# The mixer of a hybrid decoder step: column-tiled products merged into longer runs, convolution work in pairs, and the state-space decays loaded ahead

## The chip, the cores and the metric

The kernel runs on one core of a Trainium2 chip. The metric is the device time of one execution in microseconds (us). The kernel before takes 1382.97 us (median of three runs, 1382.23 to 1383.33). One of its executions was profiled; all durations below come from that execution.

## What is computed

The reference is one layer of a decoder, applied to 256 prompt tokens and to 8 sample tokens that continue cached sequences (T = 264 columns in all, D = 2048). Only the first part, the mixer, is touched. It projects the normalised input once, and the columns of the product feed two branches:

```python
proj = rms_norm(x, g_mix) @ w_in                 # [q | k | v | z | x,B,C | dt]
# sliding-window attention, 16 heads of 64, 4 key heads, chunks of 128
p = sink_softmax(logits, mask, sinks);  o = p @ v
# state-space branch (SSD), 32 heads of 64 in 4 groups, chunks of 128
xbc = silu(causal_dwconv(xbc, conv_w, conv_b))   # 24 blocks of 128 channels
la = cumsum(dt * a)
decay = exp(la[l] - la[s])                       # l >= s, else 0
y = ((cm @ bm) * decay) @ (xs * dt)              # within a chunk
y += (cm @ h_prev) * exp(la) + xs * d_skip       # from the chunk before
h = h * exp(la_end) + bm @ (xs * dt * decay_end)
y = rms_norm(y * silu(z), norm_g)
```

The concatenated branches go through an output projection. A cross-attention and a gated feed-forward network follow; they are untouched. Beside the result, the new key, value, convolution and state arrays are outputs. For the 8 sample tokens the state update is one step per token from a given state `h0`.

## The kernel before, in words

**The weight stream.** Nearly all of the time is one long stream of matrix products on TensorE (PE). Weights arrive in fp32 in parts of 1024 columns (512 KB) on the DMA queue of SyncE (SP). ScalarE (ACT) casts each part to a high half `whi` (L89), VectorE (DVE) subtracts to get the low half `wlo` (L90), and `mm3` takes three products per 128x128 block: L104 (high by high), L105 (high weights by low activations) and L106 (low weights by high activations). One part feeds 24 products of 264 columns, eight of each line. There are four buffers each for the raw part, `whi` and `wlo`, so the halves can be made at most about four parts ahead of PE, and the load of a part waits until DVE has made the `wlo` four parts earlier. `proj` (L108) walks over the parts; its results are evicted from a PSUM bank by DVE.

**Order.** Each engine executes its own instructions in one fixed order. That order is made at build time by a scheduler; weight work carries high priority, and `tc.issue_after` pins some instructions behind others. Products of the mixer's small work (attention scores, transpositions, values, SSD) stand between the products of the weight stream. PSUM has eight banks: three `mm` and two `t` for projections and small work, and one each of `s`, `x` and `y`.

**Column-tiled products.** Some small products fill only part of PE's columns (64 or 32 of 128): the values of attention (L564, L602), the sums of squares of q (L620), the transposed cumulative sums (L482) and the products of SSD within a chunk (L830). They stand in the order as uninterrupted runs of 2 to 16 instructions; an fp32 product is two instructions.

**The pieces the change touches.** `attn_first` (L568) does the first chunk of two head pairs, with a value run of 8 instructions each, called four times. `attn_prompt` (L525) does the second chunk of one head pair, called eight times, with its own value run. `attn_sample` (L671) does the sample tokens: a root (L287 on ACT, L288 on DVE), copies (L685), scores on PE (L691), maxima (L695), an exponential on ACT (L700), then values. `conv_pair` (L765) evicts two projected blocks into two of four buffers `u` (L739), copies their ends to `cnew` (L746) and convolves them (L748 on ACT, three L750 each on DVE). `ssd_prompt(g)` (L797) handles one group, chunk by chunk: it loads logs of decays by broadcast from DRAM into tiles `e` of 256 KB (L810), makes the decays on ACT (L814 for each head, L815 the exponential), multiplies by the masked product of B and C on DVE (L816), transposes `xs` on PE, runs eight products (16 instructions, L830) into bank `y`, and adds the skip term on DVE (L833, four per chunk). `ssd_sample(g)` (L866) loads states `h` and does a product and a sum for each on DVE (L874, L875). `z_pair` (L890) gates two blocks. The calls stand at L935 to L956:

```python
conv_group(0)
conv_group(1)
ssd_prompt(0)
conv_group(2)
ssd_sample(0)
ssd_prompt(1)
conv_group(3)
```

Of the kernel before, what the change touches and what calls it, by code (L numbers as in the profile page):

```python
# [48 lines left out]
def hybrid_decoder_step_kernel(ctx: ExitStack, tc: tile.TileContext, I, O):  # L49
# [26 lines left out]
    def weights(src, n=2048, into=None):  # L76

        out = []
        with tc.high_priority():
            for o in range(0, n, NPART):  # L80
                w = min(NPART, n - o)
                x = raw_part(w)
                nc.sync.dma_start(out=x, in_=src[:, o:o + w])
# [6 lines left out]
                V.tensor_tensor(out=lo, in0=x, in1=hi.bitcast(F32), op=ALU.subtract)  # L90
                out.append((hi, lo))
# [389 lines left out]
    for c in range(2):  # L481
        PE.matmul(p[0:32, 128 + c * 128:256 + c * 128], dtan[:, c, :], tri, start=True, stop=True)  # L482
# [11 lines left out]
    for i in range(4):  # L494
        u = mp.tile([128, 3 + T], F32, name=f"u{i}")
        P.memset(u[:, 0:3], 0.0)
# [3 lines left out]
    def next_u():  # L500
        ringn[0] += 1
        return ring[ringn[0] % 4]

    laT = next_u()[0:32, 3:259]
    V.tensor_copy(out=laT, in_=p[0:32, 128:384])
    nc.sync.dma_start(out=dram_la.rearrange("c h l -> h c l"), in_=laT.rearrange("p (c l) -> p c l", c=2))
# [18 lines left out]
    def attn_prompt(j, rq, nrq, c):  # L525
# [33 lines left out]
        pt = mp.tile([128, 4, 128], F32, tag="bc", name="pt", bufs=2)  # L559
        S.copy(out=pt[:, 0:2 * nb, :], in_=p[:, 0:2 * nk].rearrange("p (a q) -> p a q", q=128))  # L560
        o = psum("t")
        for h in range(2):
            for kb in range(nb):
                PE.matmul(o[64 * h:64 * h + 64, 0:128], vn[:, kb, pp, 64 * h:64 * h + 64], pt[:, h * nb + kb, :],  # L564
                          start=kb == 0, stop=kb == nb - 1)
        marks["attn"] = S.copy(out=attn[:, j, c * 128:c * 128 + 128], in_=o[:, 0:128])

    def attn_first(j):  # L568
# [29 lines left out]
        S.copy(out=pt, in_=p.rearrange("p (a q) -> p a q", q=128))  # L598
        o = psum("t")
        for i in range(4):  # L600
            h = i % 2
            PE.matmul(o[64 * h:64 * h + 64, 128 * (i // 2):128 * (i // 2) + 128], vn[:, 0, pp, 64 * h:64 * h + 64], pt[:, i, :], start=True, stop=True)  # L602
        S.copy(out=attn[:, j:j + 2, 0:128], in_=o[:, 0:256].rearrange("p (i q) -> p i q", i=2))
# [14 lines left out]
    for d in range(2):  # L618
        for j in range(4):
            PE.matmul(pq[32 * j:32 * j + 32, 0:TP], nw[:, d, :], qsq[d][:, j, :TP], start=d == 0, stop=d == 1)  # L620
# [25 lines left out]
    kl = [mp.tile([128, 2, TP], F32R, tag="e", name="kl", bufs=3) for _ in range(2)]  # L646
# [15 lines left out]

    for j in range(0, 8, 2):
        attn_first(j)
    for j in range(8):
# [3 lines left out]
        attn_prompt(j, rqs[:, :, j % 4, d:d + 2], nrqs[:, :, j % 4, d:d + 2], 1)  # L669

    def attn_sample():  # L671
# [27 lines left out]
        e = mp.tile([128, 129], F32, tag="h0", name="es_e", bufs=3)  # L699
# [7 lines left out]
        dg = mp.tile([128, 128], F32, tag="h0", name="dgs", bufs=3)  # L707
# [29 lines left out]
    def conv_blk(bi, pm):  # L737
        u = next_u()
        V.tensor_tensor(out=u[:, 3:], in0=pm, in1=r0, op=ALU.mult)  # L739
        return u  # L740

    def conv_side(b0, us, dst):
        c = mp.tile([128, 2, TP], F32, tag="c", name="c", bufs=2)
        for m, u in enumerate(us):
            bi = b0 + m
            V.tensor_copy(out=cnew[:, bi, :], in_=u[:, TP:])  # L746
# [18 lines left out]
    def conv_pair(b0, dst):  # L765
        us = []
        in_pair(lambda m, pm: us.append(conv_blk(b0 + m, pm)))
# [27 lines left out]
    xs = quarters("xs")  # L795

    def ssd_prompt(g):  # L797
        hs = slice(8 * g, 8 * g + 8)
        hp = mp.tile([128, 512], F32, tag="hp", name="hp", bufs=1)
        for c in range(2):  # L800
            cs = slice(c * 128, c * 128 + 128)
            p = psum("s")
            PE.matmul(p[:, 0:128], BT[:, g, cs], CT[:, g, cs], start=True, stop=True)
            cbm = p[:, 128:256]
            V.tensor_tensor(out=cbm, in0=p[:, 0:128], in1=tri, op=ALU.mult)
            es = []
            for hh in range(2):
                e = mp.tile([128, 4, 128], F32, tag="e", name="e", bufs=3)
                h0 = 8 * g + 4 * hh
                nc.sync.dma_start(out=e, in_=dram_la[c, h0:h0 + 4, :].partition_broadcast(128))  # L810

                with tc.issue_after(marks["attn"].ins):
                    for j in range(4):
                        S.activation(out=e[:, j, :], in_=e[:, j, :], func=AF.Relu, scale=-1.0, bias=la[:, c * 32 + h0 + j:c * 32 + h0 + j + 1])  # L814
                    S.activation(out=e, in_=e, func=AF.Exp, scale=-1.0)  # L815
                V.tensor_tensor(out=e, in0=e, in1=cbm.unsqueeze(1).broadcast_to([128, 4, 128]), op=ALU.mult)  # L816
                es.append(e)
            p = psum("x")
            for i in range(4):
                tr(p[:, i * 128:i * 128 + 128], xs[g][:, i, cs])  # L820
            xdt = mp.tile([128, 8, 64], F32, tag="xdt", name="xdt", bufs=2)
            V.tensor_tensor(out=xdt, in0=p.rearrange("p (h q) -> p h q", h=8),
                            in1=dtn[:, c, hs].unsqueeze(2).broadcast_to([128, 8, 64]), op=ALU.mult)
            xw = mp.tile([128, 8, 64], F32, tag="bc", name="xw", bufs=2)
            V.tensor_tensor(out=xw, in0=p.rearrange("p (h q) -> p h q", h=8),
                            in1=de[:, c, hs].unsqueeze(2).broadcast_to([128, 8, 64]), op=ALU.mult)
            y = psum("y")
            for h in range(8):
                o = (h % 2) * 64
                PE.matmul(y[o:o + 64, (h // 2) * 128:(h // 2) * 128 + 128], xdt[:, h, :], es[h // 4][:, h % 4, :], start=True, stop=True)  # L830
            x = xs[g][:, :, cs]
            for i in range(4):
                V.scalar_tensor_tensor(out=x[:, i, :], in0=x[:, i, :], scalar=pc("d_skip", 4 * g + i), in1=y[:, i * 128:i * 128 + 128],  # L833
                                       op0=ALU.mult, op1=ALU.add)
            if c == 1:
                yi = psum("y")
                for i in range(4):
                    PE.matmul(yi[:, i * 128:i * 128 + 128], hp[:, i * 128:i * 128 + 128], CT[:, g, cs], start=True, stop=True)
                ti = mp.tile([128, 4, 128], F32, tag="bc", name="ti", bufs=2)
                for h in range(2):  # L840
                    nc.sync.dma_start(out=ti[h * 64:h * 64 + 64], in_=lav[h][4 * g:4 * g + 4, :].partition_broadcast(64))
                S.activation(out=ti, in_=ti, func=AF.Exp)
                V.tensor_tensor(out=ti, in0=yi.rearrange("p (i l) -> p i l", i=4), in1=ti, op=ALU.mult)
                P.tensor_tensor(out=x, in0=x, in1=ti, op=ALU.add)
            st = psum("y")
            PE.matmul(st, Bn[:, c, g, :], xw.rearrange("p h q -> p (h q)"), start=True, stop=True)  # L846
            if c == 0:
                S.copy(out=hp, in_=st)
            else:
# [749 lines left out]
```

## Time and profile before

| what | value |
| --- | --- |
| median of three runs | 1382.97 us (1382.23 to 1383.33) |
| the profiled execution's own time | 1382.65 us |
| its span in the profile | 1380.6 us |
| time outside the span | 2.05 us |
| PE busy | 1375.4 us, 11415 instructions |
| DVE busy | 1050.0 us, 1865 instructions |
| ACT busy | 765.8 us, 1261 instructions |
| DMA moved | 298.32 MB, mean 216 GB/s |

A matrix product is pipelined: the profile gives each a length of about 0.28 us, but the next one starts about 0.12 us after it. What a product costs PE is therefore read from the distance between starts, not from the length in a row. In a row of the timeline stand the start, the length, the engine, the line, the operation, the tile written and the tiles read, the shape and the number of instructions; in brackets the idle time before it and what ended that. The mixer's work on which the change bears lies between about 60 and 420 us of the span.

### The profile page before, as it was taken

How to read it: one execution, taken by the hardware profiler on the slowest of the kernel's cores; microseconds unless marked ns; L12 is line 12 of the kernel's file. 1: busy time of each engine (PE TensorE's matmuls, PEld its weight loads, DVE VectorE, ACT ScalarE, POOL GpSimd, SP SyncE). 2: the span in 40 equal slices, each digit the busy share in tenths (PEclk: the TensorE clock that was granted, in tenths of full speed). 3: DMA queues.
4: the chain of work that ended last, by engine and by line, in shares of the span. 5: the costliest groups of instructions: out<-in, count | busy, mean ns of one | idle time of the engine just before them, and what ended most of it. 6: DMA issues, size and time to landing. Idle time of an engine off the chain costs nothing.

```text
span 1380.6 us, 28767 instructions
## 1 busy us (share of the span) xinstructions
PE 1375.4 (100%) x11415; PEld 1348.0 (98%) x11415; DVE 1050.0 (76%) x1865; ACT 765.8 (55%) x1261; POOL 96.1 (7%) x286
## 2 busy tenths in 40 slices
PE   9999999999999999999999999999999999999999
PEld 8999999999999999899999999999999999999998
DVE  7979799999987784579777765776577657765655
ACT  7667756556545555566565544554455445543532
POOL 0000011111000000002010000000000000000000
PEclk9999999999999999999999999999999999999999
DMA  7954468777677576865676766676567656656554
GB/s 297 333 161 134 147 209 254 228 247 256 227 230 240 185 232 213 303 235 198 190 260 214 257 215 186 212 260 213 185 214 244 198 183 198 198 183 185 193 186 139
DMA packets 89478, 298.32 MB, mean 216 GB/s; under 512 B 12032, under 2 KB 17152, under 8 KB 88832
## 3 DMA queue, kind: packets, MB, share of 16 engines
q1 hardware_dynamic: 83840, 277.61, 60.5%
q0 software_dynamic: 5504, 18.88, 4.2%
q8 instruction: 89, 1.46, 0.4%
q14 instruction: 45, 0.37, 0.1%
HBM read 280.77 MB, written 16.23 MB: 215 GB/s over the span
## 4 chain that ended last, share of the span: by engine, by line
PE 99%; DMA 0%; ACT 0%; SPq 0%; DVE 0%; issue 0%
PE mm L106 21%; PE mm L104 21%; PE mm L105 21%; PE t L106 10%; PE t L104 10%; PE t L105 10%; PE t L245 1%; PE t L283 1%; PE y L830 1%; PE y L846 0%; PE x L283 0%; DMA open<-in_open_dram 0%; PE s L245 0%; PE mm L245 0%; PE t L564 0%; PE x L1144 0%
## 5 line engine op out<-in xcount | busy, mean ns | idle before, releaser
L89 ACT CAST whi<-wraw 128x1024 fp32r<-128x1024 f32 x440 | 459.9, 1047 | 518.3 <-PE mm L105 270.2
L90 DVE TENSOR_TENSOR wlo<-wraw,whi 128x1024 fp32r<-128x1024 f32 x440 | 541.7, 1232 | 216.4 <-ACT whi L89 210.2
L106 PE MATMUL t<-x2h,wlo 128*128 128x264 f32 x704 | 198.5, 282 | 0.0
L104 PE MATMUL t<-x2h,whi 128*128 128x264 f32 x704 | 198.4, 282 | 0.0
L105 PE MATMUL t<-x2l,whi 128*128 128x264 f32 x704 | 198.4, 282 | 0.0
L105 PE MATMUL mm<-hl,whi 128*128 128x264 f32 x704 | 197.5, 282 | 0.0
L106 PE MATMUL mm<-hh,wlo 128*128 128x264 f32 x704 | 197.2, 282 | 0.0
L104 PE MATMUL mm<-hh,whi 128*128 128x264 f32 x704 | 195.7, 282 | 0.0
L104 PE MATMUL mm<-x2h,whi 128*128 128x264 f32 x672 | 189.3, 282 | 0.0
L105 PE MATMUL mm<-x2l,whi 128*128 128x264 f32 x672 | 189.3, 282 | 0.0
L106 PE MATMUL mm<-x2h,wlo 128*128 128x264 f32 x672 | 189.3, 282 | 0.0
L104 PE MATMUL mm<-xh,whi 128*128 128x264 f32 x576 | 163.7, 285 | 0.0
L105 PE MATMUL mm<-xl,whi 128*128 128x264 f32 x576 | 163.4, 285 | 0.0
L106 PE MATMUL mm<-xh,wlo 128*128 128x264 f32 x576 | 162.3, 286 | 0.0
L104 PEld LDWEIGHTS t<-x2h,whi 128*128 128x128 f32 x704 | 131.9, 187 | 0.0
L106 PEld LDWEIGHTS t<-x2h,wlo 128*128 128x128 f32 x704 | 131.9, 187 | 0.0
L105 PEld LDWEIGHTS t<-x2l,whi 128*128 128x128 f32 x704 | 131.9, 187 | 0.0
L105 PEld LDWEIGHTS mm<-hl,whi 128*128 128x128 f32 x704 | 131.9, 187 | 0.0
L106 PEld LDWEIGHTS mm<-hh,wlo 128*128 128x128 f32 x704 | 131.7, 187 | 0.0
L104 PEld LDWEIGHTS mm<-hh,whi 128*128 128x128 f32 x704 | 130.8, 187 | 0.0
L104 PEld LDWEIGHTS mm<-x2h,whi 128*128 128x128 f32 x672 | 125.9, 187 | 0.0
L105 PEld LDWEIGHTS mm<-x2l,whi 128*128 128x128 f32 x672 | 125.9, 187 | 0.0
(518 smaller groups left out, 2939.5 us busy)
## 6 DMA issues: line engine op xcount, KB each, us to landing
wraw<-in_w_up_dram SPq DMA_DIRECT2D x176, 512.0 KB, 4.2
wraw<-in_w_in_dram SPq DMA_DIRECT2D x96, 512.0 KB, 4.7
wraw<-in_w_dn_dram SPq DMA_DIRECT2D x88, 512.0 KB, 4.3
wraw<-in_w_out_dram SPq DMA_DIRECT2D x48, 512.0 KB, 4.3
h<-in_h_dram POOLq DMA_DIRECT2D x32, 256.0 KB, 4.6
hn<-in_h_dram SPq DMA_DIRECT2D x16, 512.0 KB, 4.9
out_state_s_dram<-hn POOLq DMA_DIRECT2D x16, 512.0 KB, 3.5
e<-dram_la SPq DMA_DIRECT2D x16, 256.0 KB, 4.4
```

Source lines behind the costliest of these rows:

```text
L89: S.copy(out=hi, in_=x)
L90: V.tensor_tensor(out=lo, in0=x, in1=hi.bitcast(F32), op=ALU.subtract)
L104: PE.matmul(out, wh, xh, start=start, stop=False)
L105: PE.matmul(out, wh, xl, start=False, stop=False)
L106: return PE.matmul(out, wl, xh, start=False, stop=stop)
L245: PE.matmul(first[c][:, :T], pre[k // 2][i][:, k % 2, c * 128:(c + 1) * 128], A[k // 8][x][:, k % 8, :], start=k + i + x == 0, stop=k == K ...
L283: return PE.transpose(out, in_, cst[0:k, C_ID:C_ID + k])
L830: PE.matmul(y[o:o + 64, (h // 2) * 128:(h // 2) * 128 + 128], xdt[:, h, :], es[h // 4][:, h % 4, :], start=True, stop=True)
```

## The change

1. The cumulative sums `la` are transposed once (L504) instead of being computed a second time, transposed, by the two products of L482.
2. The sums of squares of q stand in one run of 16 instructions (L640) instead of three.
3. Values: `first_values` takes two calls of `attn_first` together (two runs of 16 instructions instead of four of 8), `second_values` takes two head pairs (four runs of 16 instead of eight of 8). A run is kept whole by putting its products behind one of them with `issue_after`.
4. Convolution and gating in pairs: two buffers `u` of two blocks each, one copy to `cnew` and one to `zsam` per pair, and one tanh, one product and one gate per pair.
5. `logs()` loads the logs of a whole group into a tile `late`: two loads of 512 KB (L824) and two of the inter-chunk logs (L828), on SP. Two groups are loaded before `conv_group(1)`, the others behind the weight load that stands last at that point. The tile shares its buffers with the cached keys of `attn_sample` and other earlier tiles.
6. `ssd_prompt` takes both chunks of a group together: decays of eight heads at once (L846, L847, L848), one run of sixteen products (32 instructions, L876) into banks `y` and `s`, the skip term by ACT (L871), and an addition of 512 columns per chunk on DVE (L884). The products for the state go to bank `x`.
7. `ssd_sample(0)` is called before `conv_group(1)`; its product and sum are now L917 and L918. The operand `cb` comes in one load of 512 KB per group.

The core of the diff:

```diff
-    for i in range(4):
-        u = mp.tile([128, 3 + T], F32, name=f"u{i}")
+    for i in range(2):
+        u = mp.tile([128, 2, 3 + T], F32, name=f"u{i}")
...
-    laT = next_u()[0:32, 3:259]
-    V.tensor_copy(out=laT, in_=p[0:32, 128:384])
+    laT = next_u()[0:64, 0, 3:131]
+    p = psum("x")
+    tr(p[0:64, 0:128], la)
+    V.tensor_copy(out=laT, in_=p[0:64, 0:128])
...
+    def second_values(j, pts):
...
+        with tc.issue_after(value(1, 0, 0).ins):
+            for x in [(a, h, kb) for a in (1, 0) for h in range(2) for kb in range(2)][1:]:
+                value(*x)
+        marks["attn"] = S.copy(out=attn[:, j:j + 2, 128:TP], in_=o[:, 0:256].rearrange("p (i q) -> p i q", i=2))
...
-        e = mp.tile([128, 129], F32, tag="h0", name="es_e", bufs=3)
+        own = mp.tile([128, 512], F32, tag="hp", name="own", bufs=1)
+        e = own[:, 0:129]
...
+    def logs():
+
+        g = len(lates)
+        w = apool.tile([128, 8 * PITCH], F32, tag="B", name="late", bufs=4)
+        for c in range(2):
+            nc.sync.dma_start(out=w[:, 1024 * c:1024 * c + 1024].rearrange("p (h l) -> p h l", h=8),
+                              in_=dram_la[c, 8 * g:8 * g + 8, :].partition_broadcast(128))
+        ti = w[:, 2048:2560].rearrange("p (i l) -> p i l", i=4)
+        for h in range(2):
+            nc.sync.dma_start(out=ti[h * 64:h * 64 + 64], in_=lav[h][4 * g:4 * g + 4, :].partition_broadcast(64))
+        lates.append(w)
...
+            with tc.issue_after(marks["attn"].ins):
+                for j in range(8):
+                    S.activation(out=e[:, j, :], in_=e[:, j, :], func=AF.Relu, scale=-1.0, bias=la[:, c * 32 + 8 * g + j:c * 32 + 8 * g + j + 1])
+                S.activation(out=e, in_=e, func=AF.Exp, scale=-1.0)
+            V.tensor_tensor(out=e, in0=e, in1=cbm.unsqueeze(1).broadcast_to([128, 8, 128]), op=ALU.mult)
...
-            y = psum("y")
-            for h in range(8):
-                o = (h % 2) * 64
-                PE.matmul(y[o:o + 64, (h // 2) * 128:(h // 2) * 128 + 128], xdt[:, h, :], es[h // 4][:, h % 4, :], start=True, stop=True)
-            x = xs[g][:, :, cs]
-            for i in range(4):
-                V.scalar_tensor_tensor(out=x[:, i, :], in0=x[:, i, :], scalar=pc("d_skip", 4 * g + i), in1=y[:, i * 128:i * 128 + 128],
-                                       op0=ALU.mult, op1=ALU.add)
...
+        for i in range(4):
+            S.activation(out=xs[g][:, i, :TP], in_=xs[g][:, i, :TP], func=AF.Copy, scale=pc("d_skip", 4 * g + i))
+        ys = [psum(k) for k in ("y", "s")]
...
+        with tc.issue_after(own(1, 7).ins):
+            for c in range(2):
+                for h in range(7 if c else 8):
+                    own(c, h)
+        for c in range(2):
+            x = xs[g][:, :, c * 128:c * 128 + 128]
+            V.tensor_tensor(out=x, in0=x, in1=ys[c].rearrange("p (i l) -> p i l", i=4), op=ALU.add)
...
     conv_group(0)
+    ssd_sample(0)
+    logs()
+    logs()
     conv_group(1)
     ssd_prompt(0)
     conv_group(2)
-    ssd_sample(0)
+    with tc.issue_after(marks["load"].ins):
+        logs()
     ssd_prompt(1)
     conv_group(3)
+    with tc.issue_after(marks["load"].ins):
+        logs()
```

What this does to the order is shown at three places.

**PE, the products of SSD for group 0.** `e`, `late` are the decays, `xdt` the scaled inputs, `xh`, `xl`, `whi`, `wlo` the weight stream. In the order a product is one row or one count, on the chip it is two instructions. Before, the run of one chunk, here the second, stands alone among the products of the stream:

```order
L104 MATMUL t<-xh_77,whi 128x264
L105 MATMUL t<-xl_78,whi 128x264
L106 MATMUL t<-xh_77,wlo 128x264
L830 MATMUL y<-e,xdt 64x128 x8
L104 MATMUL t<-xh_77,whi 128x264
L105 MATMUL t<-xl_78,whi 128x264
```

After the change the sixteen products of both chunks stand together:

```order
L105 MATMUL t<-xl_78,whi 128x264
L106 MATMUL t<-xh_77,wlo 128x264
L876 MATMUL s<-late,xdt 64x128
L876 MATMUL y<-late,xdt 64x128 x8
L876 MATMUL s<-late,xdt 64x128 x7
L106 MATMUL mm<-xh_75,wlo 128x264
L104 MATMUL mm<-xh_75,whi 128x264
```

What moved: the run of the first chunk, which stood about a hundred rows earlier, is gone from there; its eight products now stand together with the second chunk's, in two banks, and one product of the second chunk leads.

**DVE, behind the copies of the sample tokens' queries.** `zz` takes those copies, `wlo` is the low half of a weight part, `sts` the softmax of the sample tokens, `h` and `ych` the sample states. Before:

```order
L685 COPY zz<-qs_sq 64x2x4x4 x4
L90 TENSOR_TENSOR wlo<-wraw,whi 128x1024
L752 SCALAR_TENSOR_TENSOR xs_2163<-xs_2163,c 128x2x256
L695 TENSOR_REDUCE sts<-s 128x1
L696 TENSOR_TENSOR sts<-sts,par 128x1
L697 TENSOR_SCALAR sts<-sts 128x1
L90 TENSOR_TENSOR wlo<-wraw,whi 128x1024
```

After:

```order
L709 COPY zz<-qs_sq 64x2x4x4 x4
L90 TENSOR_TENSOR wlo<-wraw,whi 128x1024
L773 SCALAR_TENSOR_TENSOR xs_2142<-xs_2142,c 128x2x256
L917 TENSOR_TENSOR h_2440<-h_2440,cb 128x512
L917 TENSOR_TENSOR h_2444<-h_2444,cb 128x512
L917 TENSOR_TENSOR h_2448<-h_2448,cb 128x512
L918 TENSOR_REDUCE ych<-h_2440 128x4
L90 TENSOR_TENSOR wlo<-wraw,whi 128x1024
L918 TENSOR_REDUCE ych<-h_2444 128x4
L719 TENSOR_REDUCE sts<-s 128x1
L918 TENSOR_REDUCE ych<-h_2448 128x4
L720 TENSOR_TENSOR sts<-sts,par 128x1
```

The work of the sample states now stands between the parts of the weight stream at this place; before, the first of it stood four parts later, behind the copies of L706.

**ACT, at the same place.** `qs_sq` is the root for the sample tokens, `e` and `late` the decays, `whi` the high half of a part. Before:

```order
L814 ACTIVATE e<-e,la 128x128 x4
L287 ACT_TABLE_LOAD
L287 ACTIVATE qs_sq<-t,eps 128x64
L814 ACTIVATE e<-e,la 128x128 x8
L89 CAST whi<-wraw 128x1024
L751 ACT_TABLE_LOAD
L751 ACTIVATE xs_2163<-c 128x2x256
```

After:

```order
L287 ACT_TABLE_LOAD
L287 ACTIVATE qs_sq<-t,eps 128x64
L89 CAST whi<-wraw 128x1024
L772 ACT_TABLE_LOAD
L772 ACTIVATE xs_2142<-c 128x2x256
L89 CAST whi<-wraw 128x1024 x2
L846 ACTIVATE late<-late,la 128x128 x16
L722 ACTIVATE sts<-par,sts 128x1
L725 ACTIVATE own,sts<-s,sts 128x129
L89 CAST whi<-wraw 128x1024
```

The sixteen decays of group 0 now stand in one block, behind the root, and ahead of the sample tokens' exponential (L725) and of the next cast.

More of the change, by code (lines that the diff above doesn't have):

```diff
@@ L82, in weights @@
                 x = raw_part(w)
[L83 removed]
+                marks["load"] = nc.sync.dma_start(out=x, in_=src[:, o:o + w])
                 if into:
@@ L617, in hybrid_decoder_step_kernel, with q_sums @@
     pq = psum("s")
-    for d in range(2):
-        for j in range(4):
-            PE.matmul(pq[32 * j:32 * j + 32, 0:TP], nw[:, d, :], qsq[d][:, j, :TP], start=d == 0, stop=d == 1)
+    def q_sums(d, j):
+        return PE.matmul(pq[32 * j:32 * j + 32, 0:TP], nw[:, d, :], qsq[d][:, j, :TP], start=d == 1, stop=d == 0)
+    with tc.issue_after(q_sums(1, 3).ins):
+        for d in (1, 0):
+            for j in range(4):
+                if (d, j) != (1, 3):
+                    q_sums(d, j)
     cpc = mp.tile([128, 24, 8], F32, name="cpc")
@@ L799, in ssd_prompt @@
         hp = mp.tile([128, 512], F32, tag="hp", name="hp", bufs=1)
+        late = lates[g]
+        p = psum("s")
+        es, xdts = [], []
         for c in range(2):
             cs = slice(c * 128, c * 128 + 128)
[L802 to L817, printed above, removed]
+            cbt = p[:, 256 * c:256 * c + 128]
+            cbm = p[:, 256 * c + 128:256 * c + 256]
+            PE.matmul(cbt, BT[:, g, cs], CT[:, g, cs], start=True, stop=True)
+            V.tensor_tensor(out=cbm, in0=cbt, in1=tri, op=ALU.mult)
+            e = late[:, 1024 * c:1024 * c + 1024].rearrange("p (h l) -> p h l", h=8)
+            with tc.issue_after(marks["attn"].ins):
[3 more added lines that the diff above has]
+            V.tensor_tensor(out=e, in0=e, in1=cbm.unsqueeze(1).broadcast_to([128, 8, 128]), op=ALU.mult)
+            es.append(e)
+        sts = []
+        for c in range(2):
             p = psum("x")
             for i in range(4):
-                tr(p[:, i * 128:i * 128 + 128], xs[g][:, i, cs])
+                tr(p[:, i * 128:i * 128 + 128], xs[g][:, i, c * 128:c * 128 + 128])
             xdt = mp.tile([128, 8, 64], F32, tag="xdt", name="xdt", bufs=2)
@@ L835, in ssd_prompt @@
[L835 to L849, printed above, removed]
-                hl = hp.rearrange("p (h q) -> p h q", h=8)
-                P.tensor_tensor(out=hl, in0=hl, in1=d1[:, hs].unsqueeze(2).broadcast_to([128, 8, 64]), op=ALU.mult)
-                V.tensor_tensor(out=hp, in0=hp, in1=st, op=ALU.add)
-                nc.sync.dma_start(out=O["state_p"][g], in_=hp)
+            sts.append(xw)
@@ new lines, in state, with own @@
+        def state(c):
+            st = psum("x")
+            PE.matmul(st, Bn[:, c, g, :], sts[c].rearrange("p h q -> p (h q)"), start=True, stop=True)
+            return st
+        S.copy(out=hp, in_=state(0))
+        for i in range(4):
+            S.activation(out=xs[g][:, i, :TP], in_=xs[g][:, i, :TP], func=AF.Copy, scale=pc("d_skip", 4 * g + i))
+        ys = [psum(k) for k in ("y", "s")]
+        def own(c, h):
+            o = (h % 2) * 64
+            return PE.matmul(ys[c][o:o + 64, (h // 2) * 128:(h // 2) * 128 + 128], xdts[c][:, h, :], es[c][:, h, :], start=True, stop=True)
@@ new lines, in ssd_prompt @@
+        with tc.issue_after(own(1, 7).ins):
+            for c in range(2):
+                for h in range(7 if c else 8):
+                    own(c, h)
+        for c in range(2):
+            x = xs[g][:, :, c * 128:c * 128 + 128]
+            V.tensor_tensor(out=x, in0=x, in1=ys[c].rearrange("p (i l) -> p i l", i=4), op=ALU.add)
+        yi = psum("y")
+        for i in range(4):
+            PE.matmul(yi[:, i * 128:i * 128 + 128], hp[:, i * 128:i * 128 + 128], CT[:, g, 128:256], start=True, stop=True)
```

98 lines of the change are left out of this document (54 added, 44 removed).

## The prediction

> **What bounds the kernel now.** I read the page first: the share of each engine, the granted clock, and the chain that ended last.
>
> ```profile
> span 1380.6 us, 28767 instructions
> ...
> PE 1375.4 (100%) x11415; PEld 1348.0 (98%) x11415; DVE 1050.0 (76%) x1865; ACT 765.8 (55%) x1261; POOL 96.1 (7%) x286
> ...
> PE 99%; DMA 0%; ACT 0%; SPq 0%; DVE 0%; issue 0%
> ```
>
> PE is busy for the whole span and makes 99% of the last chain. The view of waits for PE alone says whether anything else ever holds it:
>
> ```profile
> PE x L206 <- DVE eps L279: 1.2, 1, 1.2
> PE t L245 <- ACT whi L188: 0.5, 1, 0.5
> ```
>
> Two waits, 1.7 us together (columns: total, times, longest), both in the opening, which the change leaves alone. So the time is the sum of what PE executes, and a change can gain only by giving PE less to do; anything else it does can only lose, by making PE wait. The averages of the other engines hide one stage. The table of stretches (busy time of PE, PEld, DVE, ACT, POOL, then the clock, DMA share, GB/s) for the end of attention and the stage of SSD:
>
> ```profile
> core 0: us, PE busy (x) PEld busy (x) DVE busy (x) ACT busy (x) POOL busy (x), PEclk, DMA share, GB/s
> 160.00:180.00 20.00, 20.00 (x195) 19.14 (x195) 12.64 (x27) 16.55 (x34) 1.25 (x2) 1.00 0.41 123
> 180.00:259.60 79.60, 79.60 (x691) 77.68 (x690) 78.81 (x160) 42.66 (x68) 15.78 (x21) 1.00 0.74 237
> ```
>
> DVE idles 7.4 us of the first 20, and then 0.8 of 79.6. There it is as full as PE. Whether that hurts is seen at one weight part, in the timeline:
>
> ```profile
> 258.41 1.22 DVE L90 TENSOR_TENSOR wlo<-wraw,whi 128x1024 fp32r<-128x1024 f32 x1
> ...
> 260.84 0.39 PE L106 MATMUL mm<-xh,wlo 128*128 128x264 f32 x1
> ```
>
> This low half, the 66th, is done at 259.63 and first used at 260.84: DVE leads PE by 1.2 us. PE is not held, but by little. The change takes work from PE and shuffles work on DVE at this very place, so both count.
>
> **What PE saves.** First the price of a run of column-tiled instructions, from distances between starts. One run of 8 and one of 16:
>
> ```profile
> 369.25 0.28 PE L104 MATMUL mm<-ath,whi 128*128 128x264 f32 x1
> 369.37 0.28 PE L105 MATMUL mm<-atl,whi 128*128 128x264 f32 x1
> 369.58 0.66 PE L830 MATMUL y<-e,xdt 128*64 128x128 f32 x8
> 370.17 0.39 PE L104 MATMUL t<-ath,whi 128*128 128x264 f32 x1
> 370.40 0.28 PE L105 MATMUL t<-atl,whi 128*128 128x264 f32 x1
> ```
>
> ```profile
> 309.97 0.28 PE L105 MATMUL mm<-xl,whi 128*128 128x264 f32 x1
> 310.19 1.09 PE L830 MATMUL y<-e,xdt 128*64 128x128 f32 x16
> 311.21 0.39 PE L106 MATMUL mm<-xh,wlo 128*128 128x264 f32 x1
> 311.44 0.28 PE L104 MATMUL mm<-xh,whi 128*128 128x264 f32 x1
> ```
>
> A product of the stream costs 0.12 (369.25 to 369.37). From 369.37 to 370.40 are 1.03 us, less two such products 0.79 for the run of 8; from 309.97 to 311.44 are 1.47, less 0.24, so 1.23 for the run of 16. The eight further instructions cost 0.44, or 0.055 each; what is left, 0.79 - 0.44 = 0.35, is paid once a run, whatever its length. The lengths in the rows show where: the product ahead of a run is followed later, and the one behind is 0.39 long instead of 0.28.
>
> The order gives the number of runs. Products within a chunk: nine runs (seven of 16 instructions, two of 8) become four of 32, so 5 x 0.35 = 1.75. Values: four runs of 8 become two, and eight become four, 6 x 0.35 = 2.10. The instructions stay the same in number. For the sums of q and for L482 there are rows of their own:
>
> ```profile
> 79.37 0.33 PE L479 MATMUL x<-dtan,cst 128*128 128x64 f32 x2
> 79.53 0.39 PE L480 MATMUL x<-dtan,cst 128*128 128x64 f32 x2
> 79.85 0.62 PE L482 MATMUL x<-cst,dtan 128*32 128x128 f32 x4
> 80.41 0.39 PE L105 MATMUL mm<-xl,whi 128*128 128x264 f32 x1
> 80.63 0.29 PE L106 MATMUL mm<-xh,wlo 128*128 128x264 f32 x1
> ...
> 83.17 0.28 PE L105 MATMUL mm<-xl,whi 128*128 128x264 f32 x1
> 83.38 0.62 PE L620 MATMUL s<-qsq,zz 128*32 128x256 f32 x2
> 83.93 0.39 PE L106 MATMUL mm<-xh,wlo 128*128 128x264 f32 x1
> 84.16 0.28 PE L104 MATMUL mm<-xh,whi 128*128 128x264 f32 x1
> ```
>
> The lone run of 2 costs 0.99 - 0.24 = 0.75. There are two such runs beside one of 12; in one run of 16 their four instructions cost 4 x 0.055 = 0.22, so 1.50 - 0.22 = 1.28 goes. From 79.53 to 80.63 are 1.10; less 0.16 for L480 (as L479, 79.37 to 79.53) and 0.12 for L105, L482 costs 0.82. The transposition that replaces it is a whole-array product of two instructions, 0.16: 0.66 goes. Sum: 1.75 + 2.10 + 1.28 + 0.66 = 5.8 us. The bounds: if half of the 0.35 were a price of each run's first product and stayed in part, 4 us; with 0.39 a run (both lengthened ends), 6.2.
>
> Nothing else on PE changes: the stream has the same number of products. On the profiled execution, 1382.65 - 5.8 = 1376.85 (span 1374.8 and the same 2.05 outside it). The median is 0.3 above the profiled one, so 1377.2 on its scale.
>
> **What may hold PE instead.** Over the whole mixer DVE gets lighter, and its rows tell by how much:
>
> ```profile
> L874 DVE TENSOR_TENSOR h<-h,cb 128x512 f32<-128x512 f32 x32 | 22.7, 720 | 1.2 <-DMA h<-in_h_dram 1.2
> L875 DVE TENSOR_REDUCE ych<-h 128x4 f32<-128x512 f32 x32 | 21.4, 681 | 0.0
> L816 DVE TENSOR_TENSOR e<-e,s 128x512 f32<-128x512 f32 x16 | 10.6, 681 | 0.0
> L833 DVE SCALAR_TENSOR_TENSOR xs<-xs,par,y 128x128 f32<-128x128 f32 x32 | 9.2, 346 | 0.0
> ...
> L746 DVE COPY cnew<-u 128x11 f32<-128x11 f32 x24 | 4.9, 202 | 0.0
> ```
>
> The skip term's 32 x 0.346 become eight additions of 512 columns (0.68 each, as L816): 11.1 - 5.4 = 5.7 less. Twelve copies of 0.2 go: 2.4. Pairing the gates saves more, later. Since DVE is off PE's path, that is worth nothing unless DVE leads by less than zero. But the order brings work forward. Ahead of the 66th low half stood 15 L874 and 14 L875; now 22 L917 and 20 L918 do: 7 x 0.72 + 6 x 0.68 = 9.1 more. Against it, 8 skip terms become 2 additions (1.4 less), 21 copies become 11 (2.0 less), and six L816 become three of twice the size (0.5 less, at 1.2 each, estimated from 0.68 for 512 columns). Net 5.2 more ahead of that part; some parts around it have up to 9 more by the same count, some 3. PE also gets there sooner. What it saves in attention (some 4 us) DVE follows, since it stands parts ahead there and is paced by the buffers that PE frees; but of L830, three runs stood ahead of the part and now one of 32, another 3 x 1.23 - 2.11 = 1.6. So DVE is short by 5.2 + 1.6 - 1.2 = 5.6 us, and before it had 8.1 idle (7.4 + 0.8) to put this into. If it may keep no more than 2.5 idle, PE never waits. What idles DVE there is waiting, not want of work:
>
> ```profile
> 170.23 0.55 DVE L288 RECIPROCAL qs_sq<-qs_sq 128x64 f32<-128x64 f32 x1 [2.37 <-ACT qs_sq L287]
> ...
> ACT e L814 <- DMA e<-dram_la: 13.2, 6, 4.7
> ...
> L814 ACT ACTIVATE e<-e,la 128x128 f32<-128x128 f32 x64 | 20.1, 390 | 13.2 <-DMA e<-dram_la 13.2
> ```
>
> L288 waited 2.37 for a root that ACT did behind four decays; those are now behind the root, which takes perhaps half of it away. In exchange comes a new wait. Sixteen decays in a block, 16 x 0.31 (20.1 / 64) = 5.0 us of ACT, stand ahead of L725 and the next cast, and they need the `late` load. That load shares its buffer with the cached keys, so SP can issue it only after the scores L715, and every later weight load in SP's queue waits behind it. On DVE, L726 waits for L725, and behind L726 stand four operations of the sample states and a low half. A load of 256 KB made ACT wait up to 4.7 us (six times, 13.2); two of 512 KB and two smaller ones come here. DVE has some 4.6 us of other work between the low half ahead of L726 and L726 itself (L788, L917, L918, the low half) against about 6 on ACT from the same cast, so L726 costs it 1.4 if the load is in time and up to 6 if not. With 1 left of L288, 1 to 2 of waits for casts, and 1.4 to 6 for L726, DVE keeps 3.4 to 9 idle; over 2.5 that is 1 to 6.5 us for PE, and I take 3.2, nearer the lower end, since the loads start some parts ahead of use and DVE's other work is at hand. After about the 100th part the order on DVE has less ahead of each part than before, and it recovers; what PE has lost stays lost. Edits 1 and 4, `zsam` and `cnew` pairs, the `cb` load and ACT's 16 skip terms are covered by this same slack: nothing if the lead holds, inside the 3.2 if not.
>
> Forecast: 1377.2 + 3.2 = **1380.4 us**.
>
> **Rivals.** *A, the cover holds:* DVE fills its idle time with the sample states, PE never waits, and all 5.8 comes through: 1377.2. For it, 8.1 us of idle time against 5.6 needed, and the earlier root; against it, a lead of 1.2 already, and two in-order waits more. Chance 0.33.
>
> *B, slower:* the block of decays waits for its load in one piece and holds back the casts behind it. It decides once the loss exceeds 5.8. With no idle time filled (8.1) and one wait of 4.7 more, less the 2.5 allowed, PE loses 10.3: 1387.5. The 13.2 us of waits for such loads speak for it; that they held PE nowhere before, and that now there are four such blocks and not sixteen loads, against. Chance 0.07.
>
> *C, the merging doesn't pay:* the 0.35 is not a run's but a bank's or a pair's. In the run of 32, with one product in `s`, eight in `y` and seven in `s`, three stretches would pay 0.35 each, so 4 x 0.7 = 2.8 comes back, and with the 3.2 the time is 1383.2. The rows of 8 and 16 give one price for one bank; no row shows two. Chance 0.10.
>
> *D, a slower clock:* if PE stands still for long enough that its products then run at half pace, a stop of 4.7 us followed by as long at 0.24 a product loses 4.7 + 2.4, with the 3.2 of the other waits 10.3: 1387.5. Every quoted stretch has a granted clock of 1.00, and no wait of PE lasted over 1.2 us. Chance 0.02. The Trainium skill states this as a rule (TensorE: Matmul & The Clock Gate, Part 1): an idle window of about 3.4 us drops the array to half its clock; by that rule it would take one unbroken stop, and a series of short ones, as I expect, would cost nothing further; no row here is long enough to test it.
>
> **How the numbers follow.** Chances: forecast 0.48, A 0.33, C 0.10, B 0.07, D 0.02. A measurement of this kernel can tell about 0.2%, 2.8 us: faster is below 1380.2, slower above 1385.7. The forecast's own range, with a loss of 1 to 6.5, is 1378.2 to 1383.7; the part below 1380.2, a loss under 3, has about 0.13 of its 0.48. Faster: 0.33 + 0.13 = 0.46. Slower: B and D, 0.09, and 0.01 from the far end of the others. Same: the rest, 0.44. The range reaches from A with the most saved (6.2, so 1376.8) to the end of the forecast (1383.7), which takes in C and leaves B and D out.
>
> **What would show it.** Right: the four runs of 32 take 0.35 + 32 x 0.055 = 2.1 each between starts, values 1.23 a run; the view of waits for PE has new rows, L106 waiting for `wlo` of L90, all between 170 and 270 us, 2 to 6 us in all; DVE's rows have a wait of L726 for ACT. Wrong: no such row and a span near 1375 (A); a span longer by several us with one long wait for a cast, and ACT waiting for `late` ahead of it (B); a run of 32 that takes near 2.8 (C); a granted clock below 1.00 (D).

## The result, and the profile after

The changed kernel takes 1384.45 us (median of 22 runs, 1382.9 to 1386.13), the kernel before 1382.72 us (22 runs, 1381.88 to 1383.62). The ratio is 1.0014, with a 95% interval of 1.0008 to 1.0020: slower by 1.7 us, less than the 0.2% named, and 0.7 beyond the upper end of the range that was forecast. The profiled execution took 1383.68 us, with a span of 1381.9 (before 1380.6). In one thing it is not typical: its granted clock is 1.000 over the whole span, where the other 21 runs of the change have 0.997 to 0.999; the kernel before, in the 93 runs measured beside the experiments, has 1.000 in all but one (0.999).

PE's busy time fell by 4.2 us and the span grew by 1.3, so PE now waits. From the page:

```profile
span 1381.9 us, 28652 instructions
...
PE 1371.2 (99%) x11412; PEld 1347.0 (97%) x11412; DVE 1042.7 (75%) x1797; ACT 770.4 (56%) x1255; POOL 92.2 (7%) x280
...
PE 93%; DVE 3%; DMA 2%; ACT 1%; issue 1%; SPq 0%; ACTq 0%; DVEq 0%
...
late<-dram_la SPq DMA_DIRECT2D x8, 512.0 KB, 7.4
```

The chain that ended last has left PE for DVE, DMA, ACT and issue in 7% of its length; before it was 99% PE. That share is no loss by itself, since PE works beside such links; what PE loses is in its waits. The view of waits for PE has three new rows (the third row is the opening's):

```profile
PE mm L106 <- DVE wlo L90: 3.8, 2, 2.1
PE t L104 <- ACT whi L89: 1.2, 1, 1.2
PE x L206 <- DVE eps L279: 1.2, 1, 1.2
PE x L866 <- ACT hp L869: 1.0, 1, 1.0
```

Each is seen in PE's timeline as a distance between starts:

```profile
182.44 0.38 PE L283 MATMUL x<-cst,xs 128*128 128x128 f32 x2
184.50 0.39 PE L106 MATMUL mm<-xh,wlo 128*128 128x264 f32 x1 [1.69 <-DVE wlo L90]
...
187.26 0.28 PE L105 MATMUL mm<-xl,whi 128*128 128x264 f32 x1
189.62 0.39 PE L106 MATMUL mm<-xh,wlo 128*128 128x264 f32 x1 [2.08 <-DVE wlo L90]
...
209.35 0.60 PE L283 MATMUL x<-cst,xs 128*128 128x128 f32 x4
211.18 0.39 PE L104 MATMUL t<-xh,whi 128*128 128x264 f32 x1 [1.23 <-ACT whi L89]
...
275.69 0.39 PE L106 MATMUL t<-xh,wlo 128*128 128x264 f32 x1
277.06 1.12 PE L866 MATMUL x<-xw,Bn 128*128 128x512 f32 x2 [0.98 <-ACT hp L869]
```

Less what these products take by themselves (0.12 for one of the stream, about 0.22 for one transposition and 0.45 for two), PE stood still for 1.8, 2.2, 1.4 and 1.25 us, 6.7 in all. It was forecast to be 3.2.

The saving itself came. The run of 32 instructions for a group:

```profile
230.68 0.28 PE L106 MATMUL t<-xh,wlo 128*128 128x264 f32 x1
230.89 0.32 PE L876 MATMUL s<-late,xdt 128*64 128x128 f32 x1
...
232.79 0.39 PE L106 MATMUL mm<-xh,wlo 128*128 128x264 f32 x1
233.01 0.28 PE L104 MATMUL mm<-xh,whi 128*128 128x264 f32 x1
```

From 230.68 to 233.01 are 2.33, less 0.24 is 2.09 (forecast 2.1), although the run changes banks twice. By the same reading from start to start, a value run of 16 took 1.22 to 1.27 (1.23), and the one run of the sums of q (L637 in the rows) 1.28 where the three had taken 2.69: 1.4 saved (1.28). All special runs together give 5.6 us where 5.8 was summed. So 5.6 saved less 6.7 lost is 1.1 us slower; the spans differ by 1.3. These are the stops of an execution whose clock did not fall. What a lower clock costs the others can only be estimated: 0.001 of the mean clock over 1382 us is 2.8 us at half the clock, and at 0.22 a product for 0.12 (measured in e1 below) that loses 1.3 us; 0.998 to 0.999, where most of the runs lie, would be 1.3 to 2.5 us. What their stops were is not shown.

**Where the stops near 183 and 187 us come from.** Two in-order queues are held at the same time. On DVE a sample state's load comes late, with a low half behind it:

```profile
178.43 0.69 DVE L917 TENSOR_TENSOR h<-h,cb 128x512 f32<-128x512 f32 x1 [3.78 <-DMA h<-in_h_dram]
...
180.71 0.15 DVE L726 TENSOR_TENSOR sts<-sts 128x1 f32<-128x1 f32 x1
...
183.24 1.22 DVE L90 TENSOR_TENSOR wlo<-wraw,whi 128x1024 fp32r<-128x1024 f32 x1
```

On ACT the block of sixteen decays waits for the logs, with the exponential L725 and a cast behind it:

```profile
174.81 4.80 ACT L846 ACTIVATE late<-late,la 128x128 f32<-128x128 f32 x16 [3.20 <-DMA late<-dram_la]
...
179.95 0.19 ACT L725 ACTIVATION_READ_ACCUMULATOR own<-s,sts 128x1 f32 x1
180.05 1.04 ACT L89 CAST whi<-wraw 128x1024 fp32r<-128x1024 f32 x1
```

The two holds lie over each other. L726 on DVE needs L725, which ended at 180.1. Without the late state DVE would have come to L726 3.8 us sooner, at 176.9, and would have stood there until 180.1. By this estimate, from the rows, the late state cost DVE only about 0.6 us more than the block of decays would have cost it alone, so the profile cannot share the two stops out between the two; the runs below have to.

GpSimd issued the late state at 170.48, and it was used at 178.43, 7.9 us later, where such a load takes 4.7 in the middle of all; SP had issued 1.25 MB of logs from 168.29 on. And ACT has far more to do there. The groups of its decays between 180 and 259.6 us, first after, then before:

```profile
L846 ACT ACTIVATE late<-late,la 128x128 f32<-128x128 f32 x48 | 14.7, 389 | 5.2 <-DMA late<-dram_la 5.2
L847 ACT ACTIVATE late<-late 128x1024 f32<-128x1024 f32 x8 | 8.4, 1048 | 0.0
```

```profile
L814 ACT ACTIVATE e<-e,la 128x128 f32<-128x128 f32 x16 | 5.0, 389 | 6.1 <-DMA e<-dram_la 6.1
...
L815 ACT ACTIVATE e<-e 128x512 f32<-128x512 f32 x4 | 2.5, 622 | 0.0
```

L846 stands for three groups' decays and L847 for the exponentials of all four (one L847 does what two L815 did), where there was one group: 15.6 us more of ACT between the casts. ACT's busy time in this stretch rose from 42.66 to 60.25 us. The orders say the same: before, the decays stood behind the 40th to the 98th cast; now all 64 stand behind the 43rd to the 63rd.

### The profile page after: what moved, and what is told of

Same layout as the page of the kernel before. It is cut to its first block, busy times and chain, and to the rows that moved or that the text cites. A ratio compares the mean times of both kernels' runs of the same rounds, so it can differ in the third digit from the quotient of the medians.

```text
span 1381.9 us, 28652 instructions
## 1 busy us (share of the span) xinstructions
PE 1371.2 (99%) x11412; PEld 1347.0 (97%) x11412; DVE 1042.7 (75%) x1797; ACT 770.4 (56%) x1255; POOL 92.2 (7%) x280
## 4 chain that ended last, share of the span: by engine, by line
PE 93%; DVE 3%; DMA 2%; ACT 1%; issue 1%; SPq 0%; ACTq 0%; DVEq 0%
PE mm L106 19%; PE mm L104 19%; PE mm L105 19%; PE t L106 9%; PE t L104 9%; PE t L105 9%; DVE wlo L90 1%; PE t L245 1%; DMA wraw<-in_w_in_dram 1%; PE t L283 1%; DMA h<-in_h_dram 1%; PE x L866 0%; DMA late<-dram_la 0%; DVE h L917 0%; DVE c L771 0%
```

## The experiments

Three theories. **Theory 1:** the sample states (L917, L918, their loads), brought forward on DVE, make the low halves late. **Theory 2:** the loads of logs come as bursts and ACT's block waits for them. **Theory 3**, formed after the first runs: the decays of later groups, brought forward on ACT, crowd the casts. "Before" is each time the kernel before on the same chip (1382.66 to 1382.94). Whatever is edited, the scheduler makes a new order on all engines, which limits how cleanly one part is undone.

| run | median, us | ratio to before (95%) |
| --- | --- | --- |
| the change | 1384.45 | 1.0014 (1.0008 to 1.0020) |
| e1, sample states called at their old place | 1384.40 | 1.0015 (1.0006 to 1.0023) |
| e2, decays behind the sample values | 1387.53 | 1.0040 (1.0027 to 1.0052) |
| e3, both | 1386.93 | 1.0031 (1.0019 to 1.0044) |
| e4, merged runs of attention alone | 1381.64 | 0.9995 (0.9986 to 1.0004) |
| e5, no sample work on DVE | 1384.04 | 1.0012 (1.0002 to 1.0021) |
| e6, sample states later | 1380.27 | 0.9980 (0.9971 to 0.9989) |
| e7, no loads of logs | 1383.22 | 1.0006 (0.9997 to 1.0015) |
| e8, decays paced | 1382.91 | 0.9997 (0.9988 to 1.0005) |
| e9, both paced | 1380.21 | 0.9988 (0.9979 to 0.9998) |
| e10, both paced, second state in bank y | 1377.71 | 0.9962 (0.9950 to 0.9974) |
| e11, merged runs alone, sample states later | 1385.48 | 1.0017 (1.0009 to 1.0026) |
| e12, second state in bank y alone | 1385.46 | 1.0017 (1.0008 to 1.0027) |

**e1.**

```diff
     conv_group(0)
-    ssd_sample(0)
...
     conv_group(2)
+    ssd_sample(0)
```

> The changed kernel with the sample states of group 0 (L917, L918 and their loads) called where they were before the change, behind conv_group(2). Theory 1, the sample states: their work and their loads stand in VectorE's order ahead of two low halves near 180 us, one load comes 3.8 us late, and the two stops of TensorE there (1.9 and 2.2 us) go with them: about 1380.4. Theory 2, the block of decays: ScalarE still waits about 3 us for the logs of group 0 with the sample tokens' exponential and the next cast behind it, so a stop of about 2 us stays there: about 1382.5 to 1383.5.

A miss as an experiment: the order of L917 and L918 against the low halves came out the same as with the change, sum for sum, since the scheduler puts this independent work wherever DVE seems free. So it is a second sample of the change, and gives its time again. Its profile shows something else, though. Two stops, of 2.3 and 2.1 us, five apart, and behind the second the products stand 0.22 apart instead of 0.12:

```profile
188.13 0.28 PE L105 MATMUL mm<-xl,whi 128*128 128x264 f32 x1
190.50 0.46 PE L106 MATMUL mm<-xh,wlo 128*128 128x264 f32 x1 [2.10 <-DVE wlo L90]
190.76 0.42 PE L104 MATMUL mm<-xh,whi 128*128 128x264 f32 x1
190.98 0.42 PE L105 MATMUL mm<-xl,whi 128*128 128x264 f32 x1
```

The table of stretches gives the clock (third figure from the right):

```profile
190.00:192.00 2.00, 1.50 (x7) 1.50 (x8) 2.00 (x5) 1.05 (x1) 0.31 (x2) 0.67 1.27 242
192.00:194.00 2.00, 2.00 (x23) 1.72 (x25) 2.00 (x4) 0.60 (x1) 0.27 (x1) 0.50 0.58 178
```

That is rival D of the prediction, in small: a dozen products at 0.10 more, 1.2 us. The profiled execution of the change had no such stretch; it was the fifth fastest of its 22 runs. The other 21 have a mean clock below 1.000, as e1 has (0.999), so a lowered clock belongs to the change as it usually runs.

**e2 and e3.** In e2 the decays are held behind ACT's copy of the sample tokens' values; e3 adds the edit of e1.

```diff
-        S.copy(out=os_, in_=o[:, 0:128])
+        marks["attn"] = S.copy(out=os_, in_=o[:, 0:128])
```

> The changed kernel with the decays (L846, L847) held until ScalarE has copied the sample tokens' values (L740), so that neither their exponential nor a cast waits behind the load of the logs at that place. Theory 2, the block of decays: the stops near 183 and 187 us shrink to 1 us or less: about 1381 to 1382. Theory 1, the sample states: the late load of a state still holds VectorE 3.8 us, TensorE's stops stay above 3 us: 1383.5 to 1384.5.

> Both edits: sample states back at their old call and decays behind the sample tokens' values. If the two together are the cause, TensorE's stops near 183, 187 and 209 us (5.6 us) go and the saving of its runs shows: 1378.5 to 1380, with at most the stop of 1.2 us at the second product for the state left. If the paired work or the loads of 1.25 MB cost by themselves wherever they stand: 1382 or more.

Both are slower than the change, and neither theory's times were met. In e3 the call of the sample states was moved back as in e1, and as there nothing moved: DVE's order in this stage is that of e2, so e3 is a second sample of e2. In e2 the exponential L725 no longer stands behind the block (it ended at 175.7), and still DVE was held 4.0 us by a late state and PE stopped 2.65 us at 183 us: the late state is enough for that stop. The stop at 187 went. Others came some 20 us later. PE's waits in e2's timeline:

```profile
183.11 0.30 PE L283 MATMUL t<-cst,own 128*128 128x128 f32 x1 [2.65 <-DVE csm L779]
...
203.47 0.39 PE L104 MATMUL mm<-xh,whi 128*128 128x264 f32 x1 [1.28 <-ACT whi L89]
...
206.47 0.59 PE L104 MATMUL mm<-xh,whi 128*128 128x264 f32 x1 [2.50 <-DVE u L788]
...
208.79 0.59 PE L106 MATMUL mm<-xh,wlo 128*128 128x264 f32 x1 [1.51 <-DVE wlo L90]
```

With the slower clock behind them (lengths of 0.59), the three cost more than what they replaced. Only the first is a cast's: 32 decays now stood behind the 48th to 52nd cast, and those ahead of this one had waited 2.3 us for their logs. The second and third wait for DVE, which stood still here for the operand `cb` of the next sample states, ahead of L788 and a low half:

```profile
204.78 1.29 DVE L917 TENSOR_TENSOR h<-h,cb 128x512 f32<-128x512 f32 x2 [4.71 <-DMA cb<-dram_bc]
205.99 0.42 DVE L788 TENSOR_TENSOR u<-mm,r 128x264 f32<-128x264 f32 x1
```

From these runs came theory 3, that the number of decays between few casts counts, and not where the block waits; they bear it out for the stop of 1.28 at most, while the two larger ones are of the kind of theory 1, work for the sample states that waits for a load.

**e4.** The kernel before with only the values, the sums of q and the transposition of the change.

> The kernel before with the merged runs of attention alone: values in two runs of 16 and four of 16 instructions, the sums of q in one run, one transposition in place of L482; nothing of the state-space part is touched. The sum by the price of a run is 2.10 + 1.28 + 0.66 = 4.0 us less: 1378.7, with no new stop of TensorE, if VectorE follows. Rival, the price is not a run's: 1382.7. Rival, VectorE cannot follow: the gain is there until about 170 us and lost again by 260 us, 1381 to 1382.7.

The gain is 1.0 us by the medians, within its interval of none, and not 4.0. Its profile shows the rival on DVE: the products of the weight stream start 3.4 to 5 us ahead of the kernel before until 200 us, 1.5 ahead after 205, and 1.4 at the end. Between lie these waits:

```profile
PE mm L106 <- DVE wlo L90: 2.1, 3, 1.2
```

So even without the rest, a faster PE runs into DVE here. DVE must have work taken away, or moved behind this stage, before PE's saving counts.

**e5.** Leaves out the product of the sample states and sums two columns only; the loads stay.

```diff
-                V.tensor_tensor(out=h0, in0=h0, in1=cb[:, rows, :], op=ALU.mult)
-                V.tensor_reduce(out=ych[:, 4 * g + i, rows], in_=h0, op=ALU.add, axis=AX.X)
+                V.tensor_reduce(out=ych[:, 4 * g + i, rows], in_=h0[:, :, 0:2], op=ALU.add, axis=AX.X)
```

> The changed kernel with the products of the sample states (L917) left out and their sums cut to two columns; the loads stay. It leaves out part of the sample tokens' state update. Theory 1, VectorE's load: with 40 us less on VectorE between 165 and 340 us TensorE has no stop there and the whole saving of its runs shows: 1377 to 1378. Theory 2, the loads: the three waits for the logs on ScalarE, and a late load of a state, are still there, and stops of 3 us or more remain: 1380 or more.

Theory 1 in its plain form (DVE's load alone) is not enough: with DVE busy 65 of 80 us between 180 and 260, the time is that of the change within 0.4. It is not a clean test. With the buffers free at once, the state loads came still earlier (the DMA share from 160 to 180 us is 0.97, in the change 0.79), ACT waited up to 4.3 us for logs, and PE stopped in many small places, for DVE, for casts and for ACT's copy, none over 1.1 us; the profiled execution was the fastest of its ten.

**e6.** The change with each group's sample states held on DVE behind a later low half; the sums stand behind the 49th to the 104th, where the change had them behind the 41st to the 87th.

```diff
+    with tc.issue_after(marks["lo"].ins):
+        ssd_sample(0)
...
```

> The changed kernel with the sample states held on VectorE behind later weight parts (the first sum behind the 49th low half instead of the 41st, the last behind the 104th instead of the 87th; before the change 46th and 107th). Theory 1, VectorE's load ahead of each low half: the stops near 183 and 187 us fall from 4.2 to under 1.5 us, and the time to 1380 to 1381.5. Theory 2, the block of decays behind its load: ScalarE still waits 3 us there with a cast behind, the stops stay above 3 us: 1383 or more.

As theory 1 said: 4.2 us below the change, and faster than the kernel before. The first stops are gone, while ACT's wait for the logs is as long as it was:

```profile
PE x L283 <- DVE xw L860: 1.6, 1, 1.6
...
PE mm L106 <- DVE wlo L90: 0.4, 1, 0.4
...
ACT late L846 <- DMA late<-dram_la: 4.8, 2, 3.2
```

So such a wait of ACT need not hold PE when DVE is free of the sample states. Theory 2 is not refuted by this, since the new order changed ACT too:

```profile
170.62 0.35 ACT L725 ACTIVATE own<-s,sts 128x129 f32<-128x129 f32 x1
...
175.32 2.46 ACT L846 ACTIVATE late<-late,la 128x128 f32<-128x128 f32 x8 [3.19 <-DMA late<-dram_la]
177.69 1.03 ACT L89 CAST whi<-wraw 128x1024 fp32r<-128x1024 f32 x1
```

L725 now stands ahead of the waiting block, and eight decays instead of sixteen stand ahead of the next cast. Against e2, which has L725 early as well but the sample states where the change has them, e6 still shows what those states do: a stop of 2.65 us there, of 0.5 here. The largest stop left, of 1.6 at 203.69, with one of 0.4 a microsecond later, was followed by half the clock (third figure from the right):

```profile
206.00:208.00 2.00, 2.00 (x11) 2.00 (x11) 2.00 (x5) 0.61 (x1) 0.00 (x0) 0.50 0.79 234
```

The profiled execution was the slowest of its eleven; five of the others have a clock of 1.000.

**e7.** Leaves out the loads of logs; GpSimd fills the tile with a constant.

> The changed kernel without the loads of the logs (1.25 MB a group): the tile is filled with a constant by GpSimd, so the decays are not the reference's. ScalarE's block, VectorE's work and the runs stay. Theory 2, the loads: the waits of ScalarE for the logs and of VectorE for a state shrink, and the stops near 183 to 209 us fall from 5.6 to 2 us or less: 1380 to 1381. Theory 1, VectorE's load: the sample states still stand ahead of the low halves, stops of 3.5 us or more remain: 1382 to 1384.

1.2 us below the change by the medians, with overlapping runs. DVE's waits for states fell from 5.6 to 1.3 us, and of the stops up to 211 us only one of 0.7 is left, as theory 2 said. But DVE was busy 79.08 of 80 us from 180 on, PE stopped later instead (up to 1.4 us, for a cast), and the time is in the range of theory 1. So the burst has its part in the early stops, and taking it away gains little, because PE then stops elsewhere.

**e8.** The decays of a group held behind ACT's copy of the state of the group before (L869), so that their blocks stand behind the 43rd, 58th, 74th and 87th cast.

```diff
-        S.copy(out=hp, in_=state(0))
+        marks["attn"] = S.copy(out=hp, in_=state(0))
```

> The changed kernel with the decays of group g held on ScalarE behind the copy of the state (L869) of group g-1: the second, third and fourth blocks stand behind the 58th, 74th and 87th cast instead of the 49th, 56th and 63rd (before the change the decays stood behind the 40th to 98th). Theory 3, the decays brought forward crowd ScalarE's casts: the stop of 1.4 us near 211 us goes, and with it some of the later ones: 1382.5 to 1383.3. Theory 1, the sample states alone set the stops: the two near 183 and 187 us stay and the time too, 1384 to 1385.

1.5 us below the change, in the range of theory 3. The stop at 211 us and the one at L866 are gone; the two before them stayed, and are longer in the profiled execution, which was the slowest of its eleven:

```profile
186.53 0.39 PE L106 MATMUL mm<-xh,wlo 128*128 128x264 f32 x1 [3.08 <-DVE wlo L90]
...
191.64 0.59 PE L106 MATMUL mm<-xh,wlo 128*128 128x264 f32 x1 [2.08 <-DVE wlo L90]
```

**e9 and e10.** e9 has the edits of e6 and e8; e10 puts the second product for the state into bank `y` as well.

```diff
-            st = psum("x")
+            st = psum("xy"[c])
```

> The changed kernel with the sample states held on VectorE behind later weight parts and the decays of a group behind the state of the group before: both kinds of work at about the pace of the kernel before. If work brought forward on both engines is the cause, TensorE's stops fall to 1 to 2 us in all: 1378 to 1379.5. If the sample states alone matter: as with them alone, 1380.3.

> As the run before it, with the second product for the state in bank y (as before the change) instead of bank x, so that it does not wait for ScalarE's copy of the first. If that wait still costs: 0.5 to 1.2 us below the run before it; if the copy is in time once the decays are paced: the same within 0.5.

By its median e9 is what was expected if the sample states alone matter: it is no faster than e6. It spreads from 1378.0 to 1385.0 over its 12 runs, with three in the range expected of both kinds of work (the profiled one, 1378.15, is one of them); the three slowest have a clock of 0.998 to 0.999, and why it spreads so is open. e10 took 1377.26 to 1378.34 in five. It is 5.2 us faster than the kernel before, nearly the whole of PE's 5.6, and its profile has nearly nothing left of the stops:

```profile
PE t L245 <- ACT xh L166: 1.2, 1, 1.2
PE t L106 <- DVE wlo L90: 0.6, 1, 0.6
```

The first is the opening's, as is one of 1.2 left out here. ACT waited for logs here too, up to 4.6 us at a time. The row of the stage that had 74.61 of 79.6 with the change, here up to 260:

```profile
180.00:260.00 80.00, 79.36 (x658) 76.99 (x658) 76.49 (x141) 55.33 (x103) 10.71 (x14) 1.00 0.78 246
```

PE is busy 79.36 of 80 us, with DVE at 76.49 of 80. e10's advantage over e9 by the medians is 2.5 us, where 0.5 to 1.2 was expected of the bank; the profiled runs of both are equal (spans 1376.3 and 1376.5).

**e11.** e4 with the sample states held, to beyond the 110th low half.

> The kernel before with the merged runs of attention alone, and the sample states held behind later weight parts (first sum behind the 48th low half, last behind the 110th, where the run without this had 45th and 105th). Theory 1: its three stops for a low half (2.1 us) shrink, 1379 to 1380.3. If the stops come from elsewhere: 1381 to 1382.

A miss on the other side. The stops for low halves shrank from 2.1 to 0.5 us, and counted product by product e11 kept a lead of 4.4 to 4.7 us over the kernel before from 207 to 245 us, where e4 had 1.4: so it was the sample states that took e4's saving there. But the mixer's end had to wait for them instead, with a slower clock behind that (0.98 from 335 to 420 us):

```profile
PE y L300 <- DVE accy L946: 3.2, 1, 3.2
```

**e12.** The bank edit of e10 alone.

> The changed kernel with only the second product for the state in bank y instead of x. Its wait for ScalarE's copy was 1.0 us, once, in the changed kernel's profile. If that wait stands by itself: 1383.2 to 1383.8, 0.7 to 1.2 below the changed kernel, with the stops near 183, 187 and 209 us as they are. If the bank is what mattered in the run with both kinds of work paced: 1380 or less.

No gain: 1.0 us above the change. Bank `y` alone is not what made e10 fast. Whether it does anything on top of the pacing, or e10's order only leaves a little more lead than e9's, stays open, and with it how much of e10's gain is the decays'.

## Why the prediction was wrong, step by step

- **The price of a run and the sum on PE: right.** 5.6 of 5.8, with 2.09 for the run of 32. Rival C, a price for each bank, is out. The Trainium skill has the mechanism (TensorEngine Tiling (Array Packing), Key Properties): changing the tiling mode drains the array, changing the tile within a mode does not; the trace agrees, with 0.35 us once a run. Only the price is measured here, not the drain.
- **Where PE would wait: right in part.** The low halves near 183 and 187 us were named, with L725 and the next cast behind the block of decays.
- **The loss, "over 2.5 that is 1 to 6.5 us for PE, and I take 3.2, nearer the lower end": wrong,** 6.7. Of this, 4.0 fell at the two low halves, by the queue that was described. Both reasons given for the lower end failed. The loads were to "start some parts ahead of use": the block waited 3.20 us for its logs. DVE's other work was to be "at hand": a sample state's load held DVE 3.78 us ahead of L726, a wait that the sum did not have, and L726 itself then waited for nothing. In the profile the one wait hides the other. The runs show the second: e2 has the stop at 183 with L725 out of the block's way, and e6, with the states moved, has only one of 0.5 there.
- **Edits said to be covered: wrong for 2.65 us.** The stop at 211 us (a cast behind decays of group 1) and the one at 277 (L866 behind ACT's copy, in the one bank `x`) come from ACT, which the prediction looked at in one place only. It counted sixteen decays in one block, and not that all 64 had moved to between the 43rd and the 63rd cast; the order of ACT shows that without a chip. e8 bears it out for the stop at 211. The one at 277 is not the decays' directly, as the last of them were done by 252.5: the copy stood behind a cast that waited for its weight part. Why that load was late stays open.

```profile
275.48 1.05 ACT L89 CAST whi<-wraw 128x1024 fp32r<-128x1024 f32 x1 [3.42 <-DMA wraw<-in_w_in_dram]
276.43 0.58 ACT L869 COPY hp<-x 128x512 f32<-128x512 f32 x1
```

- **Rival A** ("the cover holds", 1377.2) names the time of e10, 1377.71: there the saving is nearly whole once the work that the change brought forward is spread again. **Rival B** put one long wait for a cast at the centre; in e6 ACT's wait is there (3.2), ahead of half the block and a cast, and harmless. **Rival D** is real (seen in e1, e2, e6, e8 and e11, among others), at stops shorter than was thought. With a clock below 1.000 in 21 of 22 runs it has a part in the median, 1.3 to 2.5 us by the estimate above, where the forecast put a chance of 0.02 and no price for short stops.
- Faster, same and slower stood at 0.46, 0.44 and 0.10. By the 0.2% it is "same", 1.7 us longer, where the forecast was 2.6 shorter.

## What to carry to other kernels

When a change shortens the engine that bounds the kernel, and loads data ahead, look at what the scheduler does with the work that is now ready early: here it went to the front of the other engines' in-order queues, ahead of what the bounding engine needed next. Count, for every engine that feeds the bound one, how much work stands ahead of each piece it must deliver, before and after; where the lead is near zero, work brought forward costs its own time. And look at what the brought-forward work itself waits for: in an in-order queue its load holds everything behind it. Moving the call in the source did not move the work (e1, e3); an explicit order behind a late instruction of the same engine did (e6, e8), and too late was as bad (e11).

## What the runs showed of the hardware

Stops of PE well under 3.4 us, some close together and one alone, lowered its clock. By the waits in brackets, two of 2.3 and 2.1 five apart brought it to 0.50 for about 3 us in e1, three of 1.3, 2.5 and 1.5 within six did so in e2, one of 1.6 and one of 0.4 a microsecond apart in e6, and a single one of 3.2 in e11. Yet 1.7 and 2.1 five apart in the profiled execution of the change did not, nor did the one of 2.65 in e2. The Trainium skill (TensorE: Matmul & The Clock Gate, Part 1) speaks of an idle window of about 3.4 us, running freely; by that rule none of these single stops need drop the clock, so the measurement decides. Neither the longest stop nor the sum of those close together tells the cases apart, and what does stays open. At half the granted clock the products stood 0.22 us apart, not 0.24.

A 512 KB load of logs by broadcast took 7.4 us to land (median of eight) where 256 KB before took 4.4 and a weight part of 512 KB takes 4.5.
